# Stick-breaking sums as scans along rows of keys, and a forgetting bias scanned on every partition, in a three-branch attention layer

## The chip, the core and the metric

The kernel runs on one core of one Trainium2 chip. Time is device microseconds (us) of one launch, and the median of several runs is given. The engines are TensorE (PE, with its weight loads shown as PEld), VectorE (DVE), ScalarE (ACT), GpSimd (POOL) and SyncE (SP), which issues most of the transfers.

## What is computed

One layer over 512 tokens of width 2048. A projection of the normalized input gives three attention branches of four heads of 128 channels, and merge gates. Branch A is attention with a forgetting bias, branch B attention with a bias by relative distance, branch C stick-breaking attention. Each branch output is gated, projected up, weighted by the merge gates, summed and projected once more. The parts that matter here:

```python
# A: c is the running sum of log forget gates over the tokens
logits = q @ k.T * scale + c[t, None] - c[None, s]      # masked: s <= t
p = softmax(logits)

# C: strictly causal, queries t, keys s
z  = q @ k.T * scale
lk = where(s < t, log_sigmoid(-z), 0)
r[t, s] = sum over j >= s of lk[t, j]
a  = where(s < t, exp(z + r), 0)
out = a @ v
```

## The kernel before

All activations lie channels by tokens. The large products (input projection, gates, up and output projections) are a stream of units on TensorE: 128x128 weight blocks against 512 tokens. A pair of output blocks is made by seven products over sums of halves. Each fp32 weight block is split into a rounded high part (`wh`, ScalarE, line 243) and the rest (`wl`, VectorE, line 247); the matmuls of both are line 262. The splits are made two units ahead. The same high and low split is used in attention, so a product there is three matmuls (lines 257 to 259).

A planner, the class `Flow`, fixes the order of TensorE, ScalarE and VectorE when the program is built. Each piece of work is a generator that yields engine and booked cost; at fixed places in the stream of units, `at(u, g)` starts a generator, and the planner puts its pieces between those of the stream. `t2s` counts the shared 128x512 tiles in SBUF, `atts` the four PSUM tiles of attention. At run time each engine works through its order and waits on semaphores. SP's and GpSimd's queues carry the weight loads in the order in which they were issued.

Branch C (`stick_scores`, `stick_sums`) works with keys on partitions and queries along the rows. For each of four key blocks j, of widths 512 to 128: three score matmuls; a scaled copy to `z` (line 1096); `lk` as the log of 1 + exp(-|z|) (lines 1101 to 1105) plus the positive part of z (1107), its diagonal block multiplied by a 0/1 mask (1108); a split of `lk` into `lkh` and `lkl`. When all four blocks are there, the sums over later keys run across partitions and are made on TensorE (line 1124): for block j, the high and low part of each block i >= j against a triangle of -1 (`nu_r`) or a full block of -1 (`nones_r`), and one matmul for the mask (1126). VectorE adds the sums to `z` (1135), ScalarE takes the exponential (1138), and a split gives the weights `ah`, `al`, keys on partitions, as the product with v needs them.

Branches A and B (`soft_start`, `soft_scores`, `soft_trans`) work with queries on partitions. In A the bias is a further matmul into the scores (line 1019): `crl` and `crb`, made once by `forget_sums` from one scan (line 878), hold the high and low parts of the running sums and rows of ones, and for each head ScalarE copies the rows of that head into `cr` (995). After the mask (1020), VectorE takes the row maximum (1023) and ScalarE the exponential. In B the bias is a table `tb`, loaded by SP for each head; VectorE fills a corner of it (1002) and adds it and takes the maximum in one operation (1030) with a read-out and a change of sign (1032). In both, ScalarE scales the rows, and ten transposes a head (1052) bring the weights to keys on partitions.

```python
        def stages(self):
...
            if self.n == C:
                g = [(0, one(self.plain, K)), (0, one(self.plain, Q))]
                g += [(OFF["cs"] + i, one(self.stick_scores, QB - 1 - i)) for i in range(QB)]
                g += [(OFF["ct"] + i, one(self.stick_sums, i)) for i in range(QB)]
```

Of the kernel before, what the change touches and what calls it, by code (L numbers as in the profile page):

```python
# [161 lines left out]
def hybrid_kernel(  # L162
# [123 lines left out]
    def stored(slots, n, kb):  # L286
# [23 lines left out]
    nones_r = cp.tile([P, P], F32R, name="nones_r")  # L310
    nc.vector.tensor_scalar_mul(nones_r, onef, -1.0)
# [6 lines left out]
    nc.gpsimd.affine_select(out=nu_f, in_=onef, pattern=[[-1, P]], base=0, channel_multiplier=1,  # L318
                            compare_op=ALU.is_ge, fill=0.0)
    nu_r = cp.tile([P, P], F32R, name="nu_r")  # L320
    nc.vector.tensor_scalar_mul(nu_r, nu_f, -1.0)

# [5 lines left out]
    m01 = cp.tile([P, P], F32, name="m01")  # L328
    nc.gpsimd.affine_select(out=m01, in_=onef, pattern=[[1, P]], base=0, channel_multiplier=-1,
                            compare_op=ALU.is_gt, fill=0.0)  # L330
    mskc = cp.tile([P, P], BF16, name="mskc")
    nc.gpsimd.affine_select(out=zerof, in_=zerof, pattern=[[1, P]], base=0, channel_multiplier=-1,
# [3 lines left out]
    ohf = cp.tile([P, NH], F32, name="ohf")  # L336
    nc.gpsimd.memset(ohf, 0.0)
    for r in range(4):
        nc.gpsimd.affine_select(out=ohf[32 * r:32 * r + 32, :], in_=ohf[32 * r:32 * r + 32, :],
                                pattern=[[1, NH]], base=0, channel_multiplier=-1,  # L340
                                compare_op=ALU.not_equal, fill=1.0)
# [489 lines left out]
    bias, bias_ev, f_ev, f2_ev = {}, Event(), Event(), Event()  # L831
# [36 lines left out]
    def forget_sums():  # L868
        yield f2_ev
        yield t2s, 3  # L870
        v, s, u = t2("fv"), t2("fs"), t2("fu")
        nc.gpsimd.memset(v, 0.0)
        nc.gpsimd.memset(u, 1.0)
        for r in range(4):
# [3 lines left out]
        nc.vector.tensor_tensor_scan(s, u, v, 0.0, op0=ALU.mult, op1=ALU.add)  # L878
        give(t2s)
        yield t2s, 2  # L880
        hi, lo = pair_of("c")
        yield from split(hi, lo, s, S)
        give(t2s)
        yield t2s, 2
        crl, crb = t2("crl", F32R), t2("crb")
        a = ACT, act_us(S)
        yield a
        nc.scalar.activation(crl[0:32, :], f(hi[0:32, :]), AF.Copy)
        yield a
        nc.scalar.activation(crl[32:64, :], f(lo[32:64, :]), AF.Copy)  # L890
        yield a
        nc.scalar.activation(crl[64:128, :], u[64:128, :], AF.Copy)
        nc.gpsimd.memset(crb[0:64, :], 1.0)
        yield a
        nc.scalar.activation(crb[64:96, :], f(hi[64:96, :]), AF.Copy, scale=-1.0)
        yield a
        nc.scalar.activation(crb[96:128, :], f(lo[96:128, :]), AF.Copy, scale=-1.0)
        give(t2s, 3)
        bias["crl"], bias["crb"] = crl, crb
        set_(bias_ev)  # L900

# [7 lines left out]
    class Head:  # L909
        def __init__(self, n, h, last=False):  # L910
            self.n, self.h, self.last = n, h, last
            self.prev = heads[-1] if heads else None
            heads.append(self)
            self.hl, self.z, self.lk = [None] * QB, [None] * QB, [None] * QB
            self.summed, self.lk_given = [False] * QB, []
            self.c, self.ev, self.count = {}, {}, {}
# [70 lines left out]
        def soft_start(self):  # L987
# [18 lines left out]
        def soft_scores(self, i):  # L1006
# [6 lines left out]
            yield PE, mm_us(m, 3) + (mm_us(m) + mm_us(P) if n == A else 0)  # L1013
            ps = att()[:, :m]
            mm3(ps, qh[:, blk(i)], ql[:, blk(i)], kh[:, :m], kl[:, :m], True, n == B)
            p = self.p[i]
            mx, sm = small("mx"), small("sm")
            if n == A:
                nc.tensor.matmul(ps, bias["crl"][:, blk(i)], self.bias[:, :m], start=False, stop=False)
                nc.tensor.matmul(ps[:, blk(i)], identb, mska, start=False, stop=True)  # L1020
                done = self.nth("s", QB)
                yield DVE, dve_us(m)
                nc.vector.tensor_reduce(mx, ps, axis=AX.X, op=ALU.max, negate=True)
                yield ACT, act_us(m) + 0.25
                nc.scalar.activation(p, ps, AF.Exp, bias=mx, accum_out=sm)
                give(atts)
            else:
                done = self.nth("s", QB)
                yield DVE, dve_us(m) + 0.15
                nc.vector.tensor_tensor_reduce(out=p, in0=ps, in1=self.bias[:, S - m:], scale=1.0,  # L1030
                                               scalar=-3e38, op0=ALU.add, op1=ALU.max, accum_out=mx)
                nc.vector.tensor_scalar_mul(mx, mx, -1.0)
# [25 lines left out]
        def tile_of(self, key, j, dt=F32):  # L1058

            self.tiles = getattr(self, "tiles", {})  # L1060
            if (key, j) not in self.tiles:
                t = t2(key, dt)
                self.tiles[key, j] = t[:, :S - j * P]
                if j in (1, 3):
                    self.tiles[key, 1], self.tiles[key, 3] = t[:, :S - P], t[:, S - P:]
            return self.tiles[key, j]

# [6 lines left out]
        def room_of(self, key, j, n):  # L1074
            if j in (1, 3):
                if (key, 4 - j) in self.count:
                    return
            self.count[key, j] = 1
            yield t2s, n

        def stick_scores(self, j):
            n = S - j * P
            for e in (("p", Q), ("p", K)):
                yield self.event(*e)
            yield rstd_ev
            yield from self.room_of("z", j, 1)
            yield atts, 1
            (qh, ql), (kh, kl) = self.c[Q], self.c[K]
            yield PE, mm_us(n, 3)
            ps = att()[:, j * P:]  # L1090
            mm3(ps, kh[:, blk(j)], kl[:, blk(j)], qh[:, j * P:], ql[:, j * P:], True, True)
# [9 lines left out]
            nc.vector.scalar_tensor_tensor(t, z, -1.0, z, op0=ALU.mult, op1=ALU.min)  # L1101
# [5 lines left out]
            nc.vector.scalar_tensor_tensor(t, z, 0.0, t, op0=ALU.max, op1=ALU.add)  # L1107
            nc.vector.tensor_mul(t[:, :P], t[:, :P], m01)
            yield from self.room_of("lk", j, 2)
            self.lk[j] = self.tile_of("lkh", j, F32R), self.tile_of("lkl", j, F32R)  # L1110
            yield from split(*self.lk[j], t, n, self.event("s", j))
            give(t2s)

        def stick_sums(self, j):
            n = S - j * P
            for i in range(QB):
                yield self.event("s", i)
            yield from self.parts_of(j)
            yield atts, 1
            yield PE, sum(mm_us(S - i * P, 2) for i in range(j, QB)) + mm_us(P)  # L1120
# [5 lines left out]
            nc.tensor.matmul(ps[:, blk(j)], identb, mskc, start=False, stop=True)  # L1126
# [559 lines left out]
```

## Time and profile before

| | before |
|---|---|
| median of 3 runs | 1340.83 us (1339.83 to 1341.17) |
| span of the profiled execution, first to last instruction | 1338.6 us |
| instructions | 20292 |
| TensorE matmuls in the profile | 7546 |
| lines 1124, 1126, 1019, 1020, 1052: matmuls | 80, 16, 16, 16, 80 |
| HBM read, written | 244.19 MB, 19.70 MB |

The profile is of one execution. Its own time is its span of 1338.6 us and what lies around it, which has no row; the median of the runs is 2.2 us above the span. Busy time is the union of an engine's instructions; matmuls are pipelined, so one starts before the last has ended. In rows of groups stand the line, engine, operation, output and inputs, shapes and count, then busy us and mean ns of one, then idle time of the engine just before them with what ended it. In rows of a timeline stand start and length in us, the engine, the line, and how many instructions were joined. In rows of waits stand who waited for whom, us in all, how often, and the longest.

### The profile page before, as it was taken

The page shows a single profiled execution, that of the slowest core. Times are in us where ns is not written, and L with a number is a line of the kernel's source. Part 1 is how long each engine was busy: PE and PEld are TensorE (multiplying, and loading weights), DVE is VectorE, ACT ScalarE, POOL GpSimd, SP SyncE. Part 2 cuts the span into 40 slices and gives each one's busy share as a digit, 9 for nine tenths or more (in the row PEclk, how much of TensorE's full clock was granted, in tenths as well). Part 3 has the DMA queues.
Part 4 walks back from the last instruction along what each step waited for, and adds up shares of the span by engine and source line. Part 5 has one row for each costly group of instructions (what it writes and reads, how often), then busy time and mean ns, then how long its engine had stood idle before and what let it go on. Part 6 is the DMA issues. An engine that isn't in the chain of part 4 may idle for free.

```text
span 1338.6 us, 20292 instructions
## 1 busy us (share of the span) xinstructions
PE 1326.8 (99%) x7546; PEld 1158.2 (87%) x7546; DVE 1141.3 (85%) x1691; ACT 806.2 (60%) x1274; POOL 97.9 (7%) x129
## 2 busy tenths in 40 slices
PE   8999999999999999999999999999999999999998
PEld 5888888888888888888888888888888888898887
DVE  7899888878888898888988879888888877797786
ACT  7766656556566655666567665566566645464443
POOL 0000000010100000000110100000010000000100
PEclk9999999999999999999999999999999999999999
DMA  9876677777776777777777677677777755659883
GB/s 307 231 194 163 174 190 201 184 187 181 185 218 163 209 200 182 210 175 197 201 189 190 171 203 189 183 186 189 187 182 250 281 197 177 202 152 258 239 243 103
DMA packets 92707, 265.23 MB, mean 198 GB/s; under 512 B 10528, under 2 KB 17312, under 8 KB 92608
## 3 DMA queue, kind: packets, MB, share of 16 engines
q1 hardware_dynamic: 72928, 202.77, 45.6%
q0 software_dynamic: 15552, 56.63, 25.6%
q10 hardware_dynamic: 4128, 4.53, 1.0%
q8 instruction: 59, 0.97, 0.3%
q14 instruction: 40, 0.33, 0.1%
HBM read 244.19 MB, written 19.70 MB: 197 GB/s over the span
## 4 chain that ended last, share of the span: by engine, by line
PE 96%; DVE 2%; DMA 1%; issue 0%; ACT 0%; DVEq 0%
PE acc L262 82%; PE att L262 8%; DMA raw<-in_w_col 1%; PE att L1124 1%; DVE wl L247 1%; PE att L1052 1%; PE att L257 1%; PE att L1200 1%; PE att L258 1%; PE att L1201 1%; PE att L259 1%; PE att L1199 1%; PE att L1151 0%; DVE m L247 0%; PE att L1302 0%
## 5 line engine op out<-in xcount | busy, mean ns | idle before, releaser
L247 DVE TENSOR_TENSOR wl<-raw,wh 128x1024 fp32r<-128x1024 f32 (+2 forms) x419 | 500.1, 1197 | 145.5 <-ACT wh L243 138.8
L243 ACT ACTIVATE wh<-raw 128x1024 fp32r<-128x1024 f32 (+2 forms) x419 | 434.6, 1039 | 135.6 <-PE acc L262 65.7
L262 PE MATMUL acc<-x,wh 128*128 128x512 f32 (+1 forms) x1568 | 400.5, 391 | 7.0 <-ACT wh L243 7.0
L262 PEld LDWEIGHTS acc<-x,wh 128*128 128x128 f32 x1568 | 277.3, 189 | 56.3 <-ACT wh L243 7.7
L262 PE MATMUL acc<-t,wh 128*128 128x512 f32 (+1 forms) x1128 | 282.2, 389 | 0.0
L262 PEld LDWEIGHTS acc<-t,wh 128*128 128x128 f32 x1128 | 198.5, 189 | 33.5
L262 PEld LDWEIGHTS acc<-x,wl 128*128 128x128 f32 x1504 | 207.0, 190 | 18.0 <-issue 1.7
L262 PE MATMUL acc<-x,wl 128*128 128x256 f32 (+1 forms) x1504 | 216.8, 285 | 0.6 <-DVE wl L247 0.6
L262 PEld LDWEIGHTS acc<-t,wl 128*128 128x128 f32 x1104 | 151.8, 190 | 11.4
L262 PE MATMUL acc<-t,wl 128*128 128x256 f32 x1104 | 156.2, 283 | 0.0
L282 POOL DMA_DIRECT2D raw<-in_w_col x92 | 79.7, 866 | 932.4 <-DMA raw<-in_w_col 469.0
L262 PE MATMUL acc<-m,wh 128*128 128x512 f32 (+1 forms) x512 | 114.1, 366 | 0.3 <-DVE m L247 0.2
L262 PEld LDWEIGHTS acc<-m,wh 128*128 128x128 f32 x512 | 85.4, 189 | 13.7 <-DVE m L247 1.1
L765 ACT ACTIVATE u<-acc 128x512 f32<-128x512 f32 x52 | 31.1, 599 | 75.3 <-PE acc L262 71.8
L819 ACT ACTIVATE c<-acc 128x256 f32<-128x256 f32 x51 | 19.6, 384 | 93.7 <-PE acc L262 90.6
L786 ACT ACTIVATE u<-acc 128x512 f32<-128x512 f32 x51 | 30.3, 594 | 72.7 <-PE acc L262 72.7
L635 DVE TENSOR_TENSOR raw<-raw,raw 128x1024 f32<-128x1024 f32 x54 | 65.8, 1219 | 0.4
L641 DVE TENSOR_TENSOR raw<-raw,raw 128x1024 f32<-128x1024 f32 x54 | 65.8, 1218 | 0.3
L262 PE MATMUL att<-y,wh 128*128 128x512 f32 x256 | 65.8, 389 | 0.0
L262 PEld LDWEIGHTS acc<-m,wl 128*128 128x128 f32 x448 | 60.5, 190 | 4.5 <-DVE wl L247 0.9
L262 PE MATMUL acc<-m,wl 128*128 128x256 f32 x448 | 62.6, 283 | 0.4 <-DVE wl L247 0.4
L769 ACT ACTIVATE v<-acc 128x512 f32<-128x512 f32 x52 | 31.2, 600 | 43.8 <-PE acc L262 43.3
(221 smaller groups left out, 1451.8 us busy)
## 6 DMA issues: line engine op xcount, KB each, us to landing
raw<-in_w_col SPq DMA_DIRECT2D x237, 512.0 KB, 4.5
raw<-in_w_col POOLq DMA_DIRECT2D x92, 512.0 KB, 6.8
raw<-in_w_out SPq DMA_DIRECT2D x40, 512.0 KB, 5.4
gl<-c SPq DMA_DIRECT2D x48, 256.0 KB, 4.1
raw<-in_w_up SPq DMA_DIRECT2D x32, 384.0 KB, 3.3
sg<-gl SPq DMA_DIRECT2D x48, 256.0 KB, 5.0
raw<-in_w_out POOLq DMA_DIRECT2D x16, 512.0 KB, 7.1
x<-in_xT SPq DMA_DIRECT2D x16, 256.0 KB, 7.3
```

What stands on the lines that cost most here:

```text
L243: nc.scalar.activation(hi, src, AF.Copy)
L247: nc.vector.tensor_sub(lo, src, f(hi))
L257: nc.tensor.matmul(ps, lh, rh, start=start, stop=False, skip_group_check=more)
L258: nc.tensor.matmul(ps, lh, rl, start=False, stop=False, skip_group_check=more)
L262: nc.tensor.matmul(ps, w, x, start=start, stop=stop, skip_group_check=more)
L282: nc.gpsimd.dma_start(to, src, accum_op=ALU.add)
L635: nc.vector.tensor_add(w[1], w[1], w[5])
L641: nc.vector.tensor_add(w[2], w[2], w[1])
L765: nc.scalar.activation(self.u, ps, AF.Copy)
L769: nc.scalar.activation(self.v, ps, AF.Copy)
L786: nc.scalar.activation(self.s, ps, AF.Copy)
L819: nc.scalar.activation(c, ps[:, RH], AF.Copy, scale=-1.0)
```

## The change

In branch C scores are made with queries on partitions, for query blocks i with (i + 1) x 128 keys, and the mask is added to them on TensorE. ScalarE makes |z|, exp, log, and the positive part of z in a tile of its own (`lr`). The sums over later keys then run along the row: VectorE scans it from the last key to the first, adding the two parts. VectorE subtracts the sums from `z`, ScalarE takes the exponential, and the transposes of `soft_trans` follow. The normalization is now applied to K, and the scale of a row to Q. The 20 sum matmuls of a head go.

In branch A the bias of a head is loaded from DRAM to all 128 partitions (`cb`), and VectorE scans it there with a minus sign. The term of the query is left out: it is constant along a row of the softmax. The bias is added in the operation that takes the row maximum, as in B. `forget_sums`, its tiles and constants go.

```diff
-    nones_r = cp.tile([P, P], F32R, name="nones_r")
-    nc.vector.tensor_scalar_mul(nones_r, onef, -1.0)
...
-    nu_r = cp.tile([P, P], F32R, name="nu_r")
-    nc.vector.tensor_scalar_mul(nu_r, nu_f, -1.0)
...
+    zeroc = cp.tile([P, 1], F32, name="zeroc")
+    nc.gpsimd.memset(zeroc, 0.0)
...
-    def forget_sums():
-        yield f2_ev
-        yield t2s, 3
-        v, s, u = t2("fv"), t2("fs"), t2("fu")
-        nc.gpsimd.memset(v, 0.0)
-        nc.gpsimd.memset(u, 1.0)
-        for r in range(4):
-            nc.sync.dma_start(v[32 * r:32 * r + NH, :], fd2)
-        yield Event(flow.now + 6.0)
-        yield DVE, 1.2
-        nc.vector.tensor_tensor_scan(s, u, v, 0.0, op0=ALU.mult, op1=ALU.add)
...
-        crl, crb = t2("crl", F32R), t2("crb")
...
-            if r == Q:
+            if r == K:
...
-                yield bias_ev
-                self.bias = t2("cr", F32R)
-                yield ACT, act_us(S)
-                nc.scalar.activation(self.bias, bias["crb"], AF.Copy, scale=ohf[:, self.h:self.h + 1])
+                yield f2_ev
+                self.bias = t2("cb")
+                nc.sync.dma_start(self.bias, fd2[self.h:self.h + 1, :].partition_broadcast(P))
+                yield Event(landing(flow.now, 256))
+                yield DVE, 1.3
+                nc.vector.tensor_tensor_scan(self.bias, zeroc.to_broadcast([P, S]), self.bias, 0.0,
+                                             op0=ALU.add, op1=ALU.subtract)
...
-            yield PE, mm_us(m, 3) + (mm_us(m) + mm_us(P) if n == A else 0)
+            yield PE, mm_us(m, 3) + (0.05 if n == A else 0)
             ps = att()[:, :m]
             mm3(ps, qh[:, blk(i)], ql[:, blk(i)], kh[:, :m], kl[:, :m], True, n == B)
+            if n == A:
+                nc.tensor.matmul(ps[:, blk(i)], identb, mska, start=False, stop=True)
             p = self.p[i]
             mx, sm = small("mx"), small("sm")
-            if n == A:
-                nc.tensor.matmul(ps, bias["crl"][:, blk(i)], self.bias[:, :m], start=False, stop=False)
-                nc.tensor.matmul(ps[:, blk(i)], identb, mska, start=False, stop=True)
-                done = self.nth("s", QB)
-                yield DVE, dve_us(m)
-                nc.vector.tensor_reduce(mx, ps, axis=AX.X, op=ALU.max, negate=True)
-                yield ACT, act_us(m) + 0.25
-                nc.scalar.activation(p, ps, AF.Exp, bias=mx, accum_out=sm)
-                give(atts)
-            else:
-                done = self.nth("s", QB)
-                yield DVE, dve_us(m) + 0.15
-                nc.vector.tensor_tensor_reduce(out=p, in0=ps, in1=self.bias[:, S - m:], scale=1.0,
-                                               scalar=-3e38, op0=ALU.add, op1=ALU.max, accum_out=mx)
-                nc.vector.tensor_scalar_mul(mx, mx, -1.0)
-                give(atts)
-                yield ACT, act_us(m) + 0.25
-                nc.scalar.activation(p, p, AF.Exp, bias=mx, accum_out=sm)
+            done = self.nth("s", QB)
+            yield DVE, dve_us(m) + 0.15
+            nc.vector.tensor_tensor_reduce(out=p, in0=ps, in1=self.bias[:, :m] if n == A else self.bias[:, S - m:],
+                                           scale=1.0, scalar=-3e38, op0=ALU.add, op1=ALU.max, accum_out=mx)
+            nc.vector.tensor_scalar_mul(mx, mx, -1.0)
+            give(atts)
+            yield ACT, act_us(m) + 0.25
+            nc.scalar.activation(p, p, AF.Exp, bias=mx, accum_out=sm)
...
-        def stick_scores(self, j):
-            n = S - j * P
-            for e in (("p", Q), ("p", K)):
+        def stick_start(self):
+            yield from self.turn()
+            yield t2s, 3
+            self.p = tri("z")[::-1]
+            set_(self.event("b"))
+
+        def stick_scores(self, i):
+
+            m = (i + 1) * P
+            for e in (("p", Q), ("p", K), ("b",)):
                 yield self.event(*e)
             yield rstd_ev
-            yield from self.room_of("z", j, 1)
             yield atts, 1
             (qh, ql), (kh, kl) = self.c[Q], self.c[K]
-            yield PE, mm_us(n, 3)
-            ps = att()[:, j * P:]
-            mm3(ps, kh[:, blk(j)], kl[:, blk(j)], qh[:, j * P:], ql[:, j * P:], True, True)
+            yield PE, mm_us(m, 3) + 0.05
+            ps = att()[:, :m]
+            mm3(ps, qh[:, blk(i)], ql[:, blk(i)], kh[:, :m], kl[:, :m], True, False)
+            nc.tensor.matmul(ps[:, blk(i)], identb, mskc, start=False, stop=True)
             if self.nth("s", QB):
                 give(t2s, 4)
-            z = self.z[j] = self.tile_of("z", j)
-            yield ACT, act_us(n)
-            nc.scalar.activation(z, ps, AF.Copy, scale=rcol_s[:, j:j + 1])
+            z = self.p[i]
+            yield ACT, act_us(m)
+            nc.scalar.activation(z, ps, AF.Copy, scale=rcol_s[:, i:i + 1])
             give(atts)
-            yield t2s, 1
-            t = t2("lk")[:, j * P:]
-            yield DVE, dve_us(n)
-            nc.vector.scalar_tensor_tensor(t, z, -1.0, z, op0=ALU.mult, op1=ALU.min)
-            yield ACT, act_us(n)
-            nc.scalar.activation(t, t, AF.Exp)
-            yield ACT, act_us(n)
+            yield t2s, 2
+            t, r = t2("lk")[:, :m], t2("lr")[:, :m]
+            yield ACT, act_us(m)
+            nc.scalar.activation(t, z, AF.Abs)
+            yield ACT, act_us(m)
+            nc.scalar.activation(t, t, AF.Exp, scale=-1.0)
+            yield ACT, act_us(m)
             nc.scalar.activation(t, t, AF.Ln, bias=1.0)
-            yield DVE, dve_us(n) + dve_us(P)
-            nc.vector.scalar_tensor_tensor(t, z, 0.0, t, op0=ALU.max, op1=ALU.add)
-            nc.vector.tensor_mul(t[:, :P], t[:, :P], m01)
-            yield from self.room_of("lk", j, 2)
-            self.lk[j] = self.tile_of("lkh", j, F32R), self.tile_of("lkl", j, F32R)
-            yield from split(*self.lk[j], t, n, self.event("s", j))
+            yield ACT, act_us(m)
+            nc.scalar.activation(r, z, AF.Relu)
+            yield DVE, 0.12 + 0.0022 * m
+            nc.vector.tensor_tensor_scan(t[:, ::-1], t[:, ::-1], r[:, ::-1], 0.0, op0=ALU.add, op1=ALU.add)
             give(t2s)
-
-        def stick_sums(self, j):
-            n = S - j * P
-            for i in range(QB):
-                yield self.event("s", i)
-            yield from self.parts_of(j)
-            yield atts, 1
-            yield PE, sum(mm_us(S - i * P, 2) for i in range(j, QB)) + mm_us(P)
-            ps = att()
-            for i in range(j, QB):
-                for part in self.lk[i]:
-                    nc.tensor.matmul(ps[:, i * P:], nu_r if i == j else nones_r, part,
-                                     start=i == j and part is self.lk[j][0], stop=False)
-            nc.tensor.matmul(ps[:, blk(j)], identb, mskc, start=False, stop=True)
-
-            self.summed[j] = True
-            for k, need in ((0, (0,)), (2, (0, 1, 2)), (1, (0, 1, 2, 3))):
-                if k not in self.lk_given and all(self.summed[i] for i in need):
-                    self.lk_given.append(k)
-                    give(t2s, 2)
-            a = self.z[j]
-            yield DVE, dve_us(n)
-            nc.vector.tensor_add(a, a, ps[:, j * P:])
-            give(atts)
-            yield ACT, act_us(n)
-            nc.scalar.activation(a, a, AF.Exp)
-            yield from split(*self.hl[j], a, n, self.event("a", j))
-            if self.nth("z", QB):
-                give(t2s, 3)
+            yield DVE, dve_us(m)
+            nc.vector.tensor_sub(z, z, t)
+            give(t2s)
+            yield ACT, act_us(m)
+            nc.scalar.activation(z, z, AF.Exp)
+            set_(self.event("s", i))
 
...
-                g = [(0, one(self.plain, K)), (0, one(self.plain, Q))]
-                g += [(OFF["cs"] + i, one(self.stick_scores, QB - 1 - i)) for i in range(QB)]
-                g += [(OFF["ct"] + i, one(self.stick_sums, i)) for i in range(QB)]
+                g = [(0, one(self.plain, K)), (0, one(self.plain, Q)), (OFF["cs"] - 2, self.stick_start)]
+                g += [(OFF["cs"] + i, one(self.stick_scores, i)) for i in range(QB)]
+                g += [(OFF["ct"] + i, one(self.soft_trans, i)) for i in range(QB)]
```

More of the change, by code (lines that the diff above doesn't have):

```diff
@@ L326, in hybrid_kernel @@
     nc.vector.tensor_copy(mska, nu_f)
-    m01 = cp.tile([P, P], F32, name="m01")
-    nc.gpsimd.affine_select(out=m01, in_=onef, pattern=[[1, P]], base=0, channel_multiplier=-1,
-                            compare_op=ALU.is_gt, fill=0.0)
     mskc = cp.tile([P, P], BF16, name="mskc")
-    nc.gpsimd.affine_select(out=zerof, in_=zerof, pattern=[[1, P]], base=0, channel_multiplier=-1,
+    nc.gpsimd.affine_select(out=zerof, in_=zerof, pattern=[[-1, P]], base=0, channel_multiplier=1,
                             compare_op=ALU.is_gt, fill=NEG)
     nc.vector.tensor_copy(mskc, zerof)
-    ohf = cp.tile([P, NH], F32, name="ohf")
-    nc.gpsimd.memset(ohf, 0.0)
-    for r in range(4):
-        nc.gpsimd.affine_select(out=ohf[32 * r:32 * r + 32, :], in_=ohf[32 * r:32 * r + 32, :],
-                                pattern=[[1, NH]], base=0, channel_multiplier=-1,
-                                compare_op=ALU.not_equal, fill=1.0)
+    zeroc = cp.tile([P, 1], F32, name="zeroc")
+    nc.gpsimd.memset(zeroc, 0.0)
     gq = cp.tile([P, 4], F32, name="gq")
@@ L830, in hybrid_kernel @@
     yd = {}
-    bias, bias_ev, f_ev, f2_ev = {}, Event(), Event(), Event()
+    f_ev, f2_ev = Event(), Event()
     fd, fd2 = dp.tile([NQ * NH, S], F32, name="fd"), dp.tile([NH, S], F32, name="fd2")
@@ L866, in forget_bias @@
         f2_ev.t = flow.fin + 3.0
-    def forget_sums():
-        yield f2_ev
-        yield t2s, 3
-        v, s, u = t2("fv"), t2("fs"), t2("fu")
-        nc.gpsimd.memset(v, 0.0)
-        nc.gpsimd.memset(u, 1.0)
-        for r in range(4):
-            nc.sync.dma_start(v[32 * r:32 * r + NH, :], fd2)
-        yield Event(flow.now + 6.0)
-        yield DVE, 1.2
[L878 to L884, printed above, removed]
-        crl, crb = t2("crl", F32R), t2("crb")
[L886 to L897, printed above, removed]
-        give(t2s, 3)
-        bias["crl"], bias["crb"] = crl, crb
-        set_(bias_ev)
     def tri(name, dt=F32):
@@ L913, in __init__ @@
             heads.append(self)
-            self.hl, self.z, self.lk = [None] * QB, [None] * QB, [None] * QB
-            self.summed, self.lk_given = [False] * QB, []
+            self.hl = [None] * QB
             self.c, self.ev, self.count = {}, {}, {}
@@ L1056, in soft_trans @@
             give(atts)
[L1058 to L1066, printed above, removed]
         def turn(self):
```

11 lines of the change are left out of this document (removed).

## The prediction, made before the result was known

> **What bounds the kernel now.** I read the page's busy times and chain first, then what TensorE waited for, then busy times by stage.
>
> ```profile
> span 1338.6 us, 20292 instructions
> PE 1326.8 (99%) x7546; PEld 1158.2 (87%) x7546; DVE 1141.3 (85%) x1691; ACT 806.2 (60%) x1274; POOL 97.9 (7%) x129
> PEclk9999999999999999999999999999999999999999
> PE 96%; DVE 2%; DMA 1%; issue 0%; ACT 0%; DVEq 0%
> ```
>
> ```profile
> PE acc L262 <- ACT wh L243: 7.0, 3, 6.6
> PE acc L262 <- DVE wl L247: 1.1, 2, 0.6
> PE acc L262 <- DVE m L247: 0.2, 1, 0.2
> ```
>
> ```profile
> 58.00:74.00 16.00, 14.98 (x119) 14.15 (x118) 16.00 (x23) 10.89 (x20) 0.00 (x0) 1.00 0.53 135
> 74.00:342.00 268.00, 268.00 (x1590) 238.24 (x1589) 236.27 (x363) 164.64 (x267) 21.59 (x25) 1.00 0.72 186
> 680.00:1016.00 336.00, 336.00 (x1956) 294.76 (x1955) 289.31 (x404) 213.61 (x337) 27.38 (x32) 1.00 0.71 187
> 1184.00:1205.00 21.00, 20.67 (x140) 18.41 (x138) 20.73 (x35) 9.89 (x16) 1.73 (x2) 1.00 0.65 165
> ```
>
> The stage rows give length, then busy time of PE, weight load, DVE, ACT and POOL, the granted clock, DMA share and GB/s. The stick-breaking heads (branch C) lie mostly in 74 to 342 us, the forgetting heads (branch A) in 680 to 1016. In both TensorE is busy without a gap, at full clock. All its waits in the whole run are 8.3 us, of which 6.6 is the first weight at the start. So time follows the matmul stream: a microsecond taken from TensorE in these stages comes off the end, if what TensorE reads still arrives. DVE (88% and 86% busy there) is next in line.
>
> **What TensorE loses.** "Busy" overlaps from one matmul to the next, so I price by the distance between starts. The four sum blocks of the first C head (L1124), from a block's first start to the start of its mask:
>
> ```profile
> 102.44:103.67 1.23, 1.23 (x9) 1.00 0.02 7
> 106.62:107.38 0.76, 0.76 (x7) 1.00 1.02 205
> 110.66:111.16 0.50, 0.50 (x8) 1.00 0.70 213
> 114.11:114.28 0.17, 0.17 (x3) 1.00 0.82 193
> ```
>
> Per head 20 matmuls go, 1.23 + 0.76 + 0.50 + 0.17 = 2.66 us; four heads, 10.6 us. The mask (L1126) is issued 16 times before and after, only moved from the sums to the scores: 0. The score products keep their widths (128 to 512) with queries and keys exchanged: 0. For a forgetting head, from each bias matmul (L1019) to the mask behind it:
>
> ```profile
> 742.54:742.65 0.11, 0.11 (x3) 1.00 0.95 186
> 743.13:743.25 0.12, 0.12 (x3) 1.00 0.68 137
> 743.91:744.08 0.17, 0.17 (x2) 1.00 0.73 145
> 745.72:745.95 0.23, 0.23 (x2) 1.00 1.08 214
> ```
>
> That is 0.63 us a head, 2.5 us for four.
>
> **What TensorE gains in work.** The weights of a C head now stand with queries on partitions, so each head needs the ten 128x128 transposes that branches A and B already have (L1052). From a forgetting head, and five stream matmuls behind no transpose for comparison:
>
> ```profile
> 754.48 0.60 PE L1052 MATMUL att<-identf,p 128*128 128x128 f32 x4
> 754.83 1.40 PE L262 MATMUL acc<-x,wh 128*128 128x512 f32 x5
> 756.07 1.12 PE L262 MATMUL acc<-x,wl 128*128 128x256 f32 x8
> ```
>
> ```profile
> 82.19 1.32 PE L262 MATMUL acc<-x,wh 128*128 128x512 f32 x5
> 83.34 1.12 PE L262 MATMUL acc<-x,wl 128*128 128x256 f32 x8
> ```
>
> Four transposes take 754.48 to 754.83, 0.35 us, and the five matmuls behind them 1.24 instead of 1.15: 0.44 together. So 0.11 us each, ten a head, 1.1 us; four heads, 4.4 us.
>
> [...]
>
> ```profile
> L1052 PE MATMUL att<-identf,p 128*128 128x128 f32 x80 | 13.1, 272 | 0.0
> ```
>
> 272 ns is one transpose from start to end; they start 0.09 apart and overlap. Below, the price of 272 in full is an upper bound: 40 x 0.272 = 10.9 us.
>
> **Sum.** -10.6 - 2.5 + 4.4 = -8.7 us. Span 1338.6 - 8.7 = 1329.9; the median of the runs, 1340.83, is 2.2 above the span and holds what lies around it, so 1332.1.
>
> **What must stay hidden: VectorE and ScalarE.** The groups of before:
>
> ```profile
> L1101 DVE SCALAR_TENSOR_TENSOR lk<-z 128x128 f32<-128x128 f32 (+3 forms) x16 | 7.8, 485 | 0.0
> L1107 DVE SCALAR_TENSOR_TENSOR lk<-z,lk 128x128 f32<-128x128 f32 (+3 forms) x16 | 7.7, 484 | 0.0
> L1108 DVE TENSOR_TENSOR lk<-lk,m 128x128 f32<-128x128 f32 x16 | 4.7, 292 | 0.6
> L247 DVE TENSOR_TENSOR lkl<-lk,lkh 128x128 fp32r<-128x128 f32 (+3 forms) x16 | 7.5, 484 | 0.0
> L1135 DVE TENSOR_TENSOR z<-z,att 128x512 f32<-128x512 f32 (+3 forms) x16 | 7.6, 482 | 3.5 <-PE att L1126 3.4
> L878 DVE TENSOR_TENSOR_SCAN fs<-fu,fv 128x512 f32<-128x512 f32 x1 | 1.2, 1214 | 0.0
> L1023 DVE TENSOR_REDUCE mx<-att 128x1 f32<-128x128 f32 (+3 forms) x16 | 7.5, 481 | 1.3 <-PE att L1020 1.3
> L1030 DVE CUSTOM_DVE_ANT_0 p<-att,tb 128x128 f32<-128x128 f32 (+3 forms) x16 | 7.7, 481 | 0.0
> L1030 DVE DVE_READ_ACCUMULATOR2_ANT mx<- 128x1 f32 x16 | 1.3, 82 | 0.0
> L1032 DVE TENSOR_SCALAR mx<-mx 128x1 f32<-128x1 f32 x16 | 2.5, 154 | 0.6
> ```
>
> C heads on VectorE: L1101, L1107, L1108, the low-part split and the addition go, 35.3 us; a subtraction of the same widths (7.6) and 16 scans come. A 512-wide scan took 1.214 us; at that rate per column (2.37 ns) the widths 128 to 512 make 3.03 us a head. With a fixed part they would be nearer 3.3, my value: 13.1 for four heads. Net 35.3 - 7.6 - 13.1 = 14.6 us less. No row shows a scan along a row backwards as this one is; I take it as no slower (it is the same operation on the same bytes) and bound it at twice, 26.2, where VectorE still has 1.5 us less to do.
>
> A heads on VectorE: the row maximum (7.5) becomes the addition with maximum, its read-out and the sign change (7.7 + 1.3 + 2.5), and each head scans its own row (4 x 1.21) where one scan and one split (1.2 + 0.7) served all: +7.0 us, 1.75 a head. Idle in 680 to 1016 is 336.0 - 289.3 = 46.7. The scan stands where B heads fill a corner of their bias table, and behind it wait the splits that the stream needs. How early those come, before an A head's scores:
>
> ```profile
> 726.72 1.22 DVE L247 TENSOR_TENSOR wl<-raw,wh 128x1024 fp32r<-128x1024 f32 x1
> 730.25 1.00 PE L262 MATMUL acc<-t,wl 128*128 128x256 f32 x7
> ```
>
> The split ends at 727.94, TensorE takes it at 730.25: 2.3 us of cover. The scan uses 1.2 of it, so 0; a scan later than that stalls by what exceeds 2.3.
>
> ```profile
> tb<-in_rel SPq DMA_DIRECT2D x4, 256.0 KB, 2.8
> 385.27 0.42 SPq L276 DMA_DIRECT2D tb<-in_rel  x1
> 396.28 0.11 DVE L1002 MEMSET tb<- 64x64 f32 x1
> ```
>
> The new transfer of each A head (one row of the bias to all partitions, 256 KB) goes through SP's queue like B's table, which landed 2.8 us after issue and was touched 11 us after it: some 8 us of cover, cost 0. Weight loads stand behind it in that queue in A as they do in B, where TensorE never waited. The four small loads of the removed sums go.
>
> C heads on ScalarE: the split of the stick terms goes and two passes (absolute value and positive part) come, so one pass over the widths more. As an estimate I take VectorE's pass over the same widths, 7.7 us for four heads (L1107); 268.0 - 164.6 = 103.4 is idle there. In A the per-head copy of the bias goes. But the passes ahead of the transposes now follow one another within one score stage, so this cover is the thinnest: six passes, not four, before weights that are split in the same queue.
>
> **Rivals.** (1) The new chain is late in C: copy, four ScalarE passes, scan, subtraction, exponential must end before transposes whose place in TensorE's order was fixed by the planner, and before whose end weight splits queue. For it: VectorE is already 88% busy and small passes cost more than the planner books (a 128-wide one on VectorE is booked at 0.1 + 0.00105 x 128 = 0.23 us, and L1108 took 0.292). Against: in the order of the changed program 89 matmuls of the stream lie between a head's last scores and first transposes, as many as before lay between scores and sums. A microsecond or so at each head and a little at A would give back 2 to 5 us: 1334 to 1337. (2) Transposes cost their whole 272 ns: 40 x 0.16 = 6.5 us given back, 1338.6, no change. Against: the starts above. (3) Slower: the backward scan is much slower than the forward one and VectorE becomes the bound in C. A head has 3.3 us of scans; what they take above that, less the cover of 2.3 us (read in A, taken for C too), stalls TensorE. It eats the gain of 2.2 us a head from 4.5 us more, 2.4 times as slow, a 512-wide scan of 2.9 us; at three times it is 6.6 - 2.3 = 4.3 us a head, 17.2 in all, 1349. For it: nothing seen; against: no reason in the rows. (4) The saved matmuls are not on the path because another engine takes over. Only 58 to 74 and 1184 to 1205 us show VectorE full while TensorE waits (1.0 and 0.3 us), and nothing is saved there: about 1336 if half were lost, part of case 1's range.
>
> **How the numbers follow.** Forecast 0.77, rival 1 with 4 0.13, rival 2 0.05, rival 3 0.05. A measurement of this kernel can tell 0.2%, 2.7 us, from no change. Forecast and most of rival 1 are beyond that: faster 0.89; rival 2 and the slow end of 1: same 0.06; slower 0.05. Range: below, transposes at their bare spacing of 0.09 (0.8 us less) and the two VectorE-bound stretches saving their 1.3, near 1330; above, rival 1's 1337. I take 1329.5 to 1337.
>
> **What would show it.** Right: TensorE's busy time near 1318 with the same three short waits; transposes of C at 0.11 between starts; no L1124 or L1019; VectorE's busy time about 7.6 lower; scans of 512 at 1.2 us. Wrong: a wait of TensorE for a VectorE or ScalarE line between 74 and 342 us (rival 1, or 3 if the 512-wide scan reads 2.9 us or more), transposes 0.27 apart (2), or a scan of A waiting for its transfer.

## The result, and the profile after the change

| | before | after |
|---|---|---|
| median of the runs, us | 1340.99 (1339.83 to 1341.17, 4 runs) | 1331.33 (1330.74 to 1333.40, 4 runs) |
| ratio after / before | | 0.9934, 95% interval 0.9921 to 0.9946 |
| span of the profiled execution, us | 1338.6 | 1329.7 |
| TensorE busy, us | 1326.8 | 1317.4 |
| VectorE busy, us | 1141.3 | 1134.5 |
| ScalarE busy, us | 806.2 | 806.3 |

The kernel is 0.66% faster. The page of the changed kernel, its first lines and the head of the chain that ended last:

```profile
span 1329.7 us, 20204 instructions
PE 1317.4 (99%) x7490; PEld 1149.0 (86%) x7490; DVE 1134.5 (85%) x1675; ACT 806.3 (61%) x1280; POOL 94.8 (7%) x120
PE 98%; DVE 1%; DMA 0%; issue 0%; ACT 0%; DVEq 0%
```

Its waits of TensorE (total, times, longest):

```profile
PE acc L262 <- ACT wh L243: 6.8, 2, 6.6
PE acc L262 <- DVE m L247: 1.5, 2, 1.3
PE acc L262 <- DVE wl L247: 0.6, 1, 0.6
```

These are the three waits of before, 8.9 us against 8.3, and no new one. The span is 8.9 us shorter, TensorE's busy time 9.4. The 56 matmuls fewer are 80 sums and 16 bias products gone and 40 transposes come. Both attention stages still have no gap (length, then busy time of PE, weight load, DVE, ACT and POOL, clock, DMA share, GB/s):

```profile
74.00:342.00 268.00, 268.00 (x1584) 235.69 (x1584) 230.97 (x323) 173.82 (x288) 22.39 (x26) 1.00 0.70 188
680.00:1007.00 327.00, 327.00 (x1899) 287.21 (x1898) 284.77 (x417) 200.73 (x314) 25.89 (x30) 1.00 0.73 193
```

VectorE is busy 231.0 us of the first stage, where it was 236.3; ScalarE 173.8, where it was 164.6.

The scans among VectorE's groups (busy time, mean ns of one), C's with all four widths together, then the 512-wide ones of C and of A by themselves:

```profile
L1045 DVE TENSOR_TENSOR_SCAN lk<-lk,lr 128x128 f32<-128x128 f32 (+3 forms) x16 | 13.1, 819 | 1.3 <-ACT lr L1043 1.3
```

```profile
L1045 DVE TENSOR_TENSOR_SCAN lk<-lk,lr 128x512 f32<-128x512 f32 x4 | 4.9, 1220 | 0.2 <-ACT lr L1043 0.2
L948 DVE TENSOR_TENSOR_SCAN cb<-zeroc,cb 128x512 f32<-128x512 f32 x4 | 4.9, 1219 | 0.0
```

C's sixteen scans take 13.1 us; the backward scan of 512 columns (L1045, 1220 ns) costs what the forward one does (L948, 1219). How the transposes stand in TensorE's order, two blocks of the first C head (start, length, operation):

```profile
102.58 0.60 PE L998 MATMUL att<-identf,z 128*128 128x128 f32 x4
102.93 1.40 PE L262 MATMUL acc<-x,wh 128*128 128x512 f32 x5
104.17 1.12 PE L262 MATMUL acc<-x,wl 128*128 128x256 f32 x8
105.83 0.49 PE L998 MATMUL att<-identf,z 128*128 128x128 f32 x3
106.08 1.40 PE L262 MATMUL acc<-x,wh 128*128 128x512 f32 x5
107.32 1.11 PE L262 MATMUL acc<-x,wl 128*128 128x256 f32 x8
```

Four take 0.35 us to the next start, three take 0.25; the five matmuls behind them take 1.24 instead of the 1.15 of before. That is 0.11 each, as for branch A's before.

**A cleaner distance.** The first attention score starts anywhere from 73.06 to 76.32 us in the traces below, by what happens in the start stage, which no kernel here changes. So I also compare the distance from that start to the start of the last group of the matmul stream. Before:

```profile
75.12 0.22 PE L257 MATMUL att<-qkh,qkh 128*128 128x128 f32 x1
...
1334.09 1.12 PE L262 MATMUL acc<-m,wl 128*128 128x256 f32 x8
```

After:

```profile
74.79 0.22 PE L257 MATMUL att<-qkh,qkh 128*128 128x128 f32 x1
...
1325.17 1.12 PE L262 MATMUL acc<-m,wl 128*128 128x256 f32 x8
```

1258.97 and 1250.38: 8.59 us less, where the sum of the prediction was 8.7. The other 0.3 of the span is the start. In a second profiled execution of the changed kernel the distance was 1250.39 (74.86 to 1325.25), so here the reading repeats to hundredths, while the times of the runs scatter by 1 to 3 us.

### The profile page after: what moved, and what is told of

It is laid out like the page before. It is cut to its first block, busy times and chain, and to the rows that moved or that the text cites. A ratio compares the mean times of both kernels' runs of the same rounds, so it can differ in the third digit from the quotient of the medians.

```text
span 1329.7 us, 20204 instructions
## 1 busy us (share of the span) xinstructions
PE 1317.4 (99%) x7490; PEld 1149.0 (86%) x7490; DVE 1134.5 (85%) x1675; ACT 806.3 (61%) x1280; POOL 94.8 (7%) x120
## 4 chain that ended last, share of the span: by engine, by line
PE 98%; DVE 1%; DMA 0%; issue 0%; ACT 0%; DVEq 0%
PE acc L262 84%; PE att L262 8%; PE att L998 1%; PE att L257 1%; PE att L258 1%; PE att L1111 1%; PE att L1112 1%; PE att L259 1%; PE att L1110 1%; DVE wl L247 0%; PE att L1062 0%; DMA raw<-in_w_col 0%; PE att L1213 0%; PE att L899 0%; PE att L900 0%; DVE m L247 0%
## 5 line engine op out<-in xcount | busy, mean ns | idle before, releaser
L262 PEld LDWEIGHTS acc<-t,wl 128*128 128x128 f32 x1104 | 151.7, 190 | 11.4
L627 DVE TENSOR_TENSOR raw<-raw,raw 128x1024 f32<-128x1024 f32 x54 | 65.9, 1220 | 0.5
L621 DVE TENSOR_TENSOR raw<-raw,raw 128x1024 f32<-128x1024 f32 x54 | 65.9, 1220 | 0.4
L262 PEld LDWEIGHTS att<-y,wh 128*128 128x128 f32 x256 | 48.1, 188 | 10.0
```

The source lines that it names most:

```text
L262: nc.tensor.matmul(ps, w, x, start=start, stop=stop, skip_group_check=more)
L621: nc.vector.tensor_add(w[1], w[1], w[5])
L627: nc.vector.tensor_add(w[2], w[2], w[1])
```

## The experiments

Theory: TensorE's stream sets the time, and what counts is the distance between its starts. Each experiment has its own measurement of the kernel before, 1340.24 to 1340.30 us; the ratios refer to it.

**Branch A alone.** The forgetting heads as in the changed kernel, the stick-breaking heads as before. Diffs here are against the changed kernel, and show a part of the edit; `...` marks what is left out.

```diff
...
-                g = [(0, one(self.plain, K)), (0, one(self.plain, Q)), (OFF["cs"] - 2, self.stick_start)]
-                g += [(OFF["cs"] + i, one(self.stick_scores, i)) for i in range(QB)]
-                g += [(OFF["ct"] + i, one(self.soft_trans, i)) for i in range(QB)]
+                g = [(0, one(self.plain, K)), (0, one(self.plain, Q))]
+                g += [(OFF["cs"] + i, one(self.stick_scores, QB - 1 - i)) for i in range(QB)]
+                g += [(OFF["ct"] + i, one(self.stick_sums, i)) for i in range(QB)]
```

> Branch A changed alone, branch C as before. Theory (time follows the matmul stream): only the 16 bias matmuls (L1019 before, 2.60 us from start to next start) leave TensorE, so about 2.6 us below before, 1338.4, with TensorE's short waits as before. Rival (the gain of the whole change came from the relief of VectorE in branch C, 14.6 us by the sum): here VectorE gets 7.0 us more and nothing less, so no gain, 1341 to 1348.

Measured: 1337.24 us (1335.83 to 1339.65, 11 runs), ratio 0.9981, interval 0.9972 to 0.9990. Its timeline of TensorE, first score and last stream group:

```profile
73.51 0.22 PE L257 MATMUL att<-qkh,qkh 128*128 128x128 f32 x1
...
1329.76 1.12 PE L262 MATMUL acc<-m,wl 128*128 128x256 f32 x8
```

1256.25, so 2.72 us less than before; the prediction had 2.5. VectorE is busy 1145.8 us there, 4.5 more than before, and the kernel is faster all the same: relief of VectorE is not where A's gain comes from.

**Branch C alone.** The stick-breaking heads as in the changed kernel; the sums of the bias and its matmul as before.

```diff
-                yield f2_ev
-                self.bias = t2("cb")
-                nc.sync.dma_start(self.bias, fd2[self.h:self.h + 1, :].partition_broadcast(P))
...
+                yield bias_ev
+                self.bias = t2("cr", F32R)
+                yield ACT, act_us(S)
+                nc.scalar.activation(self.bias, bias["crb"], AF.Copy, scale=ohf[:, self.h:self.h + 1])
```

> Branch C changed alone, branch A as before. Theory: 80 sum matmuls go (10.56 us from start to next start), 40 transposes come (10.48 - 6.61 = 3.87 us by the same measure), so 6.7 us below before, 1334.3. Rival (relief of VectorE): VectorE has 14.6 us less here, more than in the whole change, so at least its 9.7 us, 1331 or less.

Measured: 1334.87 us (1333.62 to 1336.63, 5 runs), ratio 0.9963, interval 0.9949 to 0.9977. First score and last stream group:

```profile
74.06 0.22 PE L257 MATMUL att<-qkh,qkh 128*128 128x128 f32 x1
...
1327.19 1.12 PE L262 MATMUL acc<-m,wl 128*128 128x256 f32 x8
```

1253.13, so 5.84 us less than before, where the prediction had 10.6 - 4.4 = 6.2. The two parts add up, 2.72 + 5.84 = 8.56 of 8.59: neither takes or gives the other anything. The rival's 1331 or less for C alone did not come.

**Each transpose of C twice.** It measures the price of 40 transposes by themselves.

```diff
-                nc.tensor.transpose(ps[:, blk(i)], self.p[i][:, blk(j)], identf)
+                for _ in range(2 if self.n == C else 1):
+                    nc.tensor.transpose(ps[:, blk(i)], self.p[i][:, blk(j)], identf)
```

> The changed kernel with each of the 40 transposes of branch C issued twice into the same place; nothing else differs and the output is the same. Theory: a transpose costs the distance between starts, 0.10 to 0.11 us, so 4.0 to 4.4 us above the changed kernel, 1335.3 to 1335.7. Rival (a transpose costs the 0.272 us that its row shows): 10.9 us more, 1342.2.

Measured: 1336.94 us (11 runs), ratio 0.9975, interval 0.9966 to 0.9984; 5.6 above the changed kernel, but the two were measured apart. The same kernel again, beside a repeat of the changed one on one chip:

> The changed kernel itself, as the measure for the three others on the same chip: 1331.3 by the first measurement, 1330.7 to 1333.4; by the theory 8.9 us (the drop of the span) below before.

> The doubled transposes of branch C beside the changed kernel on one chip, since the first look compared kernels of two chips (5.6 us apart, 4.8 us by TensorE's busy time). Theory: 4.4 to 4.8 us above the changed kernel. Rival (full 0.272 us each): 10.9.

Measured: 1331.46 us (1330.98 to 1332.80, 5 runs) for the changed kernel and 1336.81 (1335.22 to 1337.08, 8 runs) for the doubled transposes. Timeline of TensorE with doubled transposes: a wait in the start stage, the first score, a block, the last group:

```profile
59.73 2.17 PE L262 MATMUL acc<-x,wh 128*128 128x256 f32 x16 [0.95 <-ACT wh L243]
...
76.13 0.22 PE L257 MATMUL att<-qkh,qkh 128*128 128x128 f32 x1
...
103.92 1.03 PE L999 MATMUL att<-identf,z 128*128 128x128 f32 x8
104.71 1.39 PE L262 MATMUL acc<-x,wh 128*128 128x512 f32 x5
...
1330.87 1.12 PE L262 MATMUL acc<-m,wl 128*128 128x256 f32 x8
```

Eight transposes take 0.79 us where four took 0.35. First score to last group is 1254.74, 4.35 more than in the changed kernel beside it: 4.35 / 40 = 0.11 us each. The 5.35 between the medians holds that and about 1 us of the start, where this profile shows a wait of 0.95 that the changed kernel's does not. The whole 272 ns, 10.9 us, is refuted by both.

**The scan of C twice, and three times.** Extra scans of the same operands into a spare tile, ahead of the real one, not booked with the planner, so that the order of the instructions stays. The second kernel has `range(2)` there.

```diff
+            for _ in range(1):
+                nc.vector.tensor_tensor_scan(scrap[:, :m][:, ::-1], t[:, ::-1], r[:, ::-1], 0.0, op0=ALU.add, op1=ALU.add)
             nc.vector.tensor_tensor_scan(t[:, ::-1], t[:, ::-1], r[:, ::-1], 0.0, op0=ALU.add, op1=ALU.add)
```

> The changed kernel with each of the 16 scans of branch C preceded by the same scan into a spare tile, not booked in the planner: 13.1 us more work for VectorE in the order as it stands. Theory: 3.3 us a head, of which the cover of 2.3 us and idle time hide most; 0 to 1.0 us a head, 1331.3 to 1335.3. Rival (VectorE sets the time): all 13.1 us, 1344.4.

Measured: 1334.80 us (1334.05 to 1337.36, 5 runs), ratio 0.9962, interval 0.9950 to 0.9975; VectorE busy 1145.8. TensorE has two waits that the changed kernel does not have:

```profile
PE att L999 <- ACT z L1054: 1.4, 1, 1.4
...
PE att L259 <- DVE qkl L247: 0.3, 1, 0.3
```

First score to last group is 1253.44 (74.41 to 1327.85): 13.1 us of scans more on VectorE cost 3.1. Of these, 1.7 are the two new waits (transposes for the exponential, 1.4; a score for a split, 0.3); where the other 1.4 lie the waits do not say.

> As with the doubled scans, but two extra scans ahead of each: 26.2 us more for VectorE, as if a backward scan took three times as long. Theory of the prediction's third rival: 6.6 us more a head, less 2.3 us of cover, 4.3 us a head, 17 us above the changed kernel, 1348. If the idle time between the splits hides more than the cover of one split, less: the 14.6 us that branch C took off VectorE and the wait of its order would leave 0 to 8 us, 1331 to 1339.

Measured: 1350.10 us (1348.01 to 1352.07, 5 runs), ratio 1.0072, interval 1.0059 to 1.0085. Its waits of TensorE:

```profile
PE acc L262 <- ACT wh L243: 6.7, 1, 6.7
PE acc L262 <- DVE wl L247: 5.2, 6, 1.6
PE acc L262 <- ACT v L756: 3.2, 3, 2.1
PE att L999 <- ACT z L1054: 2.7, 2, 1.5
PE acc L262 <- DVE m L247: 1.5, 2, 1.3
PE acc L262 <- ACT u L773: 0.9, 1, 0.9
```

Its stages with C heads, the granted clock in the third column from the end:

```profile
74.00:120.00 46.00, 42.96 (x256) 37.42 (x255) 43.98 (x70) 30.34 (x57) 3.43 (x4) 0.96 0.63 161
120.00:160.00 40.00, 35.84 (x191) 30.42 (x190) 37.53 (x57) 24.00 (x44) 2.58 (x3) 0.91 0.58 151
290.00:342.00 52.00, 49.68 (x281) 42.40 (x280) 46.76 (x64) 33.64 (x58) 4.32 (x5) 0.97 0.62 164
```

Now the weight splits come late (5.2 us against 0.6), then copies and transposes behind them. The new waits are 4.6 + 3.2 + 2.7 + 0.9 = 11.4 us. Beside them the clock falls short by 0.04 x 46 + 0.09 x 40 + 0.03 x 52 = 7.0 us of full speed. Together 18.4 of the 18.7 us that the span is longer than the changed kernel's (1348.4 against 1329.7). The distance from the first score to the last group is 20.4 longer (73.06 to 1343.90), since the first score came earlier here; 2.0 of that are in neither. VectorE is close to full in C by then, busy 43.98 of 46.00 us in the first row and 37.53 of 40.00 in the second, while TensorE stands still for 3.0 and 4.2 us.

**The mask of C on VectorE.** If starts on TensorE are all that counts, the 16 mask matmuls are worth what they take there, and an addition of 128x128 on VectorE in their place costs nothing.

```diff
-            nc.tensor.matmul(ps[:, blk(i)], identb, mskc, start=False, stop=True)
...
             nc.scalar.activation(z, ps, AF.Copy, scale=rcol_s[:, i:i + 1])
             give(atts)
+            yield DVE, dve_us(P)
+            nc.vector.tensor_add(z[:, blk(i)], z[:, blk(i)], mskc)
```

> The changed kernel with the mask of branch C added by VectorE to the diagonal block of z after the scaled copy, in place of 16 bf16 matmuls. Theory (time follows the stream; a mask matmul costs 0.04 us to the next start and about 0.1 us in the start of the matmul behind it): 16 x 0.14 = 2.2 us less, 1329.1, with 16 x 0.29 = 4.7 us more for VectorE hidden. Rival (a mask costs only its 0.04 us): 0.6 us less, 1330.7. Rival (VectorE's 4.7 us show): 1331 to 1336.

Measured: 1330.54 us (1330.06 to 1331.05, 5 runs), ratio 0.9927, interval 0.9914 to 0.9941. Timeline of TensorE, start wait, first score, last group:

```profile
59.92 2.17 PE L262 MATMUL acc<-x,wh 128*128 128x256 f32 x16 [1.56 <-ACT wh L243]
...
76.32 0.22 PE L257 MATMUL att<-qkh,qkh 128*128 128x128 f32 x1
...
1324.84 1.12 PE L262 MATMUL acc<-m,wl 128*128 128x256 f32 x8
```

1248.52, 1.9 less than the changed kernel; 0.12 us a mask. But the start came 1.5 us later, with a wait of 1.56 ahead of all attention, and little is left in the time. Run again beside the changed kernel:

> The mask of branch C on VectorE, beside the changed kernel on one chip. In the first look TensorE's busy time fell by 1.9 us and a wait of 1.56 us for the weights at 60 us, ahead of all attention, took most of it back. Theory: that wait varies from run to run and the median is 1.9 to 2.2 us below the changed kernel. Rival (the wait belongs to the kernel): 0 to 0.8 us below.

Measured: 1330.85 us (1329.96 to 1331.26, 5 runs) against 1331.46: 0.6 lower, with ranges that overlap. That is the number of the rival, but not its cause: this time the start wait was not there, and the distance was still only 0.35 less (75.02 to 1325.06). What took most of the rest is under the last heading.

**The masks of C and of A on VectorE.** In A the mask goes into the bias row on all partitions, blocks from last to first.

```diff
-            if n == A:
-                nc.tensor.matmul(ps[:, blk(i)], identb, mska, start=False, stop=True)
...
+                if i < QB - 1:
+                    yield self.event("m", i + 1)
+                yield DVE, dve_us(P)
+                nc.vector.tensor_add(self.bias[:, blk(i)], self.bias[:, blk(i)], mska)
```

> As before it, and in branch A too: VectorE adds the mask to the diagonal block of the bias row, block by block from the last query block to the first, so that no block has to be restored; all 32 mask matmuls of A and C go. Theory: 32 x 0.14 = 4.5 us below the changed kernel, 1326.8. Rival (only 0.04 us each): 1.3 us, 1330.0. Rival (the longer VectorE chain of A, where a block's mask waits for the addition before it, makes TensorE wait for the transposes): 1329 to 1333.

Measured: 1332.85 us (1332.48 to 1333.68, 5 runs), ratio 0.9947, interval 0.9934 to 0.9959: a miss, slower than the changed kernel by 1.5. Timeline of TensorE in the last A head:

```profile
1038.51 0.50 PE L1116 MATMUL att<-ah,vl 128*128 128x512 f32 x1 [1.06 <-DVE vl L1077]
...
1041.85 0.49 PE L262 MATMUL att<-y,wh 128*128 128x512 f32 x1 [1.44 <-ACT y L243]
```

The blocks depend on one another through the bias tile, and in the last head, behind which nothing of the stream is left to fill in, the longer chain ends in two new waits, 2.5 us. A loss of clock in a late stage, as under the last heading, comes on top (0.92 over 1175 to 1196 us, 1.7 us). Left as in the changed kernel for that head alone:

> Masks of branch C and of the first three heads of A on VectorE; the last A head keeps its mask on TensorE and its order of blocks, because in the look before its longer VectorE chain let TensorE wait 2.7 us at 1038 to 1043 us. Theory: 28 masks x 0.12 to 0.14 us = 3.4 to 3.9 us below the changed kernel and no waits there. Rival (VectorE's chain in the other A heads shows too): not below mask_c.

Measured: 1330.36 us (1327.67 to 1331.02, 5 runs), ratio 0.9923, interval 0.9911 to 0.9936. The waits in A are gone. Distance 1248.45 (76.27 to 1324.72), 1.9 less than the changed kernel, and 3.6 less but for 1.7 us of clock that it lost in a late stage (last heading), where 28 masks at 0.12 are 3.4; median 1.1 less, within the scatter. None of these versions is shown to beat the changed kernel.

## Why the prediction was right, step by step

- **What bounds the kernel: right.** TensorE is the chain (98%), and what was taken from its starts came off the end: 8.6 us of 8.7. The median, 1331.33, lies 0.8 below the 1332.1 of the sum, within what the runs scatter. A part of that is the 2.2 us that were added to the span: they are the difference between a median and the span of one execution. The profiled execution of the changed kernel took 1331.46, 1.8 above its own span.
- **Bias matmuls, 2.5: right**, 2.7 with all of A's change.
- **Sums less transposes, 6.2: right to 0.4**, 5.8 by C alone. The term of the transposes, 4.4, holds. Blocks of four and of three cost 0.11 for each transpose alike (the rows above). Added up over the trace, the 40 take 3.3 us to the next starts, and behind 13 of their 16 blocks the matmuls of the stream take 0.09 longer, 1.2 us (behind the other three stand transposes of another tile): 4.5. The 4.35 us for 40 more fits that. Mis-sized is the term of the moved mask, put at 0. A mask, too, lengthens the matmuls of the stream behind it. The five matmuls that the prediction shows at 82.19 as standing behind no transpose have a mask of C ahead of them in the changed kernel, and take 1.24 to the next row instead of 1.15:

```profile
82.06 0.23 PE L1027 MATMUL att<-mskc,identb 128*128 128x128 bf16 x1
82.09 1.40 PE L262 MATMUL acc<-x,wh 128*128 128x512 f32 x5
83.33 1.12 PE L262 MATMUL acc<-x,wl 128*128 128x256 f32 x8
```

Before, the stream followed 11 of C's 16 masks directly, and now it follows all 16 (13 times with 512 columns, at 0.09, and three times with 256, at 0.06): 1.4 us against 1.0, while the masks' own starts take 0.1 us less. So the move costs about 0.3 us, and 10.6 - 4.5 - 0.3 = 5.8. This is added up from the traces; no run moves the masks alone.
- **The 272 ns that a transpose lasts were not its price.** The mean of C's 40 is 272 ns here too (L998), and they overlap with what follows: doubling them cost 0.11 us each. The granted clock was 1.00 in the stage that holds them (74 to 342 us); no block of transposes is longer than 0.79 us here, and a longer run of them was not tried.
- **VectorE, 7.6 less: 6.8, in part by luck.** The scans of C are 13.1 as predicted, and backward is as fast as forward (1220 and 1219 ns at 512 columns). But by the branches alone C takes 11.2 us of busy time off VectorE (1130.1 against 1141.3), where the sum had 14.6, and A adds 4.5, where it had 7.0. Both terms were added up from the busy times of rows, and neighbouring instructions overlap: of the 35.3 us that go in C, only 28.2 are time in which VectorE runs nothing else, and of the 20.8 that come, 17.5. The two errors nearly cancel.
- **Cover of VectorE: 2.3 us a head, about right; the bound "at twice" was read wrongly.** I noted that with scans twice as long VectorE "still has 1.5 us less to do" than before. That kernel lost 3.1 us all the same: total work does not say what is late. The other rule of the prediction, a stall of what exceeds 3.3 + 2.3 us a head, gives 4 x (6.6 - 5.6) = 4 us at twice (3.1 measured) and 17.2 at three times, 1349 (1350.1). The second agreement is partly luck: 11.4 us were waits, the other 7.0 a loss of clock that the rule does not know. Rival 3 was a mechanism that exists, with a condition that did not come.
- **The transfer of A: cost 0 right, size off.** I took 2.8 us to land, as B's table of the same 256 KB. One row sent to all partitions (`cb`) takes 5.1, by the transfers of the changed kernel (KB each, median us to landing):

```profile
cb<-fd SPq DMA_DIRECT2D x4, 256.0 KB, 5.1
```

The first is issued at 717.4 and its scan starts at 728.4, so 5.9 us of cover remain where I had some 8.
- **ScalarE, 7.7 more in C: nearly right**, 6.0 by C alone (812.2 us busy against 806.2). The 9.2 between the stage's windows compares stretches that do not hold the same work. Over the whole run it is even: A alone takes 5.8 off (800.4), since its copies are gone.
- **Rivals.** 1: no wait for a line of the new chain, refuted. 2: refuted by the doubled transposes. 4: the late VectorE-bound stage gave back 0.14 us, not half of the gain. Its listed waits grew from 0.3 to 1.5 us, but the first and last of the same fourteen matmul groups, before and after, are 20.68 and 20.82 apart:

```profile
1184.75 1.60 PE L262 MATMUL acc<-m,wh 128*128 128x256 f32 x12
...
1205.43 0.73 PE L262 MATMUL acc<-m,wl 128*128 128x256 f32 x4 [0.45 <-DVE wl L247]
```

```profile
1175.78 1.60 PE L262 MATMUL acc<-m,wh 128*128 128x256 f32 x12
...
1196.60 1.12 PE L262 MATMUL acc<-m,wl 128*128 128x256 f32 x8
```

## What to carry to other kernels

Where one engine has no gap, price an edit by the distance between starts on it, not by the duration of the instructions: here the sum then came out to 0.1 us (8.7 against 8.59), while the duration of the transposes, 10.9 us, would have left 2.2 of the gain. Count an instruction that is only moved, too: here five stream matmuls behind a mask took 1.24 us, and 1.15 without it. For the other engines ask how much later a result may come, not whether their total work falls. When a saving of a microsecond or two is to be judged, read it between two fixed instructions of the trace, since the start of the run scattered by as much here (first score at 73.06 to 76.32 us), and look at the granted clock between them (0.94 against 1.00 over 30 us cost 1.8).

## What the runs showed of the hardware that was not expected

**Behind a short wait the clock was halved in some executions.** In the untouched stage near 1186 us the changed kernel and its versions with masks moved have the same wait of 1.3 us. The windows of 30 us around it, first in the repeat with C's mask on VectorE, then in the changed kernel beside it:

```profile
1170.00:1200.00 30.00, 28.52 (x191) 26.49 (x191) 25.82 (x40) 13.78 (x20) 1.73 (x2) 0.94 0.64 175
```

```profile
1170.00:1200.00 30.00, 28.53 (x204) 26.64 (x203) 27.23 (x44) 14.49 (x22) 1.73 (x2) 1.00 0.65 170
```

The busy time is the same, but the clock is 0.94 against 1.00: 30 x 0.06 = 1.8 us, about the 1.5 that the repeat of the mask experiment missed (0.35 instead of 1.9). The first mask experiment ran the same kernel, and its trace has 1.00 in this window, so the program alone does not decide it. In the kernel with C's and three A heads' masks moved, closer, a window and then its timeline of TensorE:

```profile
1185.70:1189.10 3.40, 3.40 (x15) 3.30 (x16) 3.40 (x7) 0.20 (x1) 0.53 (x1) 0.50 0.66 193
```

```profile
1185.56 1.36 PE L262 MATMUL acc<-m,wh 128*128 128x256 f32 x5 [1.30 <-DVE m L247]
1186.71 1.91 PE L262 MATMUL acc<-m,wl 128*128 128x256 f32 x8
```

Eight matmuls that elsewhere take 1.11 us take 1.91, at a clock of 0.50 over 3.4 us (3.4 x 0.5 = 1.7 us lost), behind a wait of 1.30. Three of the eleven traces with this wait have such a stretch (the repeat with C's mask moved and both with A's, 0.94 over the 30 us in each), the other eight have none. What decides it was not tried. The clock that the tripled scans lost comes in short stretches too. Of the six windows from 74 to 342 us, the three shown above have 0.96, 0.91 and 0.97, and the other three 1.00. In the second of those shown, the matmuls are slow from 150.69 to 156.45, eight again at 1.91, behind waits of 1.21 and 1.52:

```profile
148.72 0.33 PE L999 MATMUL att<-identf,z 128*128 128x128 f32 x1 [1.21 <-ACT z L1054]
150.56 0.47 PE L999 MATMUL att<-identf,z 128*128 128x128 f32 x1 [1.52 <-ACT z L1054]
150.69 2.48 PE L262 MATMUL acc<-x,wh 128*128 128x512 f32 x5
152.97 1.91 PE L262 MATMUL acc<-x,wl 128*128 128x256 f32 x8
154.68 1.48 PE L262 MATMUL acc<-t,wh 128*128 128x512 f32 x3
155.96 0.74 PE L999 MATMUL att<-identf,z 128*128 128x128 f32 x3
156.45 1.41 PE L262 MATMUL acc<-t,wh 128*128 128x512 f32 x5
```

**A mask costs three times its own spacing.** Taking the 16 bf16 mask matmuls of C away saved 1.9 us, 0.12 each, where in the changed kernel the next matmul starts 0.04 us after a mask (0.64 us for 16, added up over the trace). The rest lies in the matmuls behind, as with the transposes: five of them at 82.09 take 1.24 us instead of 1.15.
